# A hybrid encoder layer on one core: attention gates before the attention loop, memory queries and keys inside it, and the turn of the gates' maxima pinned within head 0

## The chip, the core and the metric

The kernel runs on one core of a Trainium2 chip. Its engines, as the profile names them, are PE (TensorE, the matrix multiplier), DVE (VectorE), ACT (ScalarE), POOL (GpSimd) and SP (SyncE, which here issues nearly all DMAs). Matmul results land in PSUM banks, all other tiles lie in SBUF. The metric is the device time of one execution in microseconds (us); the median of three is 2049.92.

## What is computed

Two sequences of 512 tokens, x_prompt and x_sample, of width 1024, go through the same layer in fp32. Cut to what matters here:

```python
x = x + 0.5 * swiglu(rms_norm(x, ffn1_norm), ffn1_w_gate, ffn1_w_up, ffn1_w_down)
h = rms_norm(x, mix_norm)
aq, ak, av, mq, mk, mv, gate_pre, o_pre, g_att, g_mlstm = jnp.split(h @ w_in, split_at, axis=-1)
aq = apply_rope(rms_norm(aq.reshape(B, S, 8, 64), q_norm), cos, sin)   # 8 heads
ak = apply_rope(rms_norm(ak.reshape(B, S, 2, 64), k_norm), cos, sin)   # 2 key heads
att = gqa_block_attention(aq, ak, av)                                  # softmax(q k / 8) v
mem = mlstm_bidirectional(mq, mk, mv, gate_pre, mlstm_gate_bias, o_pre, mlstm_head_norm)  # 4 heads of 128
merged = sigmoid(g_att) * (att @ w_up_att) + sigmoid(g_mlstm) * (mem @ w_up_mlstm)
x = x + merged @ w_out
x = x + 0.5 * swiglu(rms_norm(x, ffn2_norm), ffn2_w_gate, ffn2_w_up, ffn2_w_down)
```

The names to keep: **g_att** (attention gates, 8 blocks of 128 columns), **mq and mk** (memory queries and keys, 4 heads), **o_pre** (output gates, 4 heads) and **gate_pre** (16 columns of input and forget gates, from which running maxima are taken). `mlstm_bidirectional` is a gated linear attention in both directions, here computed in blocks of 128 tokens with those maxima as stabilizers.

## The kernel before

**Arithmetic.** A product of two fp32 matrices is made of three matmuls on pairs (hi, lo): hi x hi, hi x lo, lo x hi. So every operand that comes out of a computation is *split* (L712 to L714): ACT copies it to hi, DVE subtracts hi from it to get lo.

**Stages.** The first feed-forward network (both sequences), then `mix(s, ...)` (L837) once for each *stream* s: s=0 is x_prompt, s=1 is x_sample. Then the second network and the final norm. `mix` is a generator; the main program runs the first stream up to its output projection, starts the second stream's first projections, and lets the rest of the first stream's output projection run while the second stream prepares its queries. The tiles of mixing are 128 rows (columns of a weight) by 512 tokens.

**Units.** Nearly all projections of `mix` are *units* of 24 matmuls (8 blocks of the width times 3), each with 128 columns of w_in: `out_gate(h)` for o_pre, `att_gate(d)` for g_att, `mem_gate(d)` for g_mlstm, `mem_qk(h, j)` for mq (j=0) and mk (j=1). What follows a unit's last matmul differs:

- `mem_qk`: in the first stream DVE multiplies by R, the norm's factor of each token (L1013), then a split (ACT copy, DVE L714). In the second stream the input is already normed, and the split reads PSUM directly. The result lies in a tile of tag w8 in the first stream (the buffers of split weights, 4 of them) and of tag wr in the second (the buffers of weights as they come from memory, 4 of them).
- the gates (`gate_of`, L858 to L861): in the first stream DVE multiplies by R (L860), then ACT takes tanh; in the second ACT alone. An attention gate is written into `mg[:, d, :]`. The blocks `mg[:, 4:8, :]` hold the raw queries until these are turned, so gates 4 to 7 come after the last query turn.

**Weights.** `load_w` (L284): in the first stream a weight is fetched (L271), split by ACT (L278) and DVE (L279, one instruction of 128 x 1024), and both halves are written back to memory (*parked*, L301). In the second stream the parked halves are read (L293) and nothing is split. One unit's weights are always loaded ahead of its matmuls: `go` and `among` hold the next unit (`held`) while they compute one.

**From the queries to the attention loop.** After the projections of keys, values and queries stands the first yield of `mix`; between it and the second come `gates()` (L945: log-sigmoids, cumulative sums, one transpose, running maxima on DVE), the rotation of the first queries, `k_turn` (keys transposed by PE into a PSUM bank, then copied and subtracted by ACT and DVE, L928 to L931), `q_turn(0)` (L1029) and `gate_tops` (L982 to L986): two small transposes by PE of the maxima, 32 rows each (L984, L985), copied to SBUF by DVE. Turns take their bank from one pool of two (tile name pst). Around these stand four units, one before the first yield, three after the second.

**The attention loop.** 8 heads (h) of four steps (b). `score` (L1079) makes 128 x 512 scores with two matmuls, DVE takes the row maximum (L1086), ACT the exponential, DVE the reciprocal (L1089), and DVE or ACT scales the row (L1093, L1091). `turn_keys` (L1096) transposes a 128-column block of the four score tiles by four PE transposes (L1099) and splits the result. `values` (L1106) multiplies with the values. The scores of head h+1 are made while head h is turned, the values one step behind. In between, `among(n)` runs n matmuls of units one by one from the queue:

```python
if h + 1 < HA:
    nxt.append(score(h + 1, b))
among(FILLER[0])            # 5
pp = turn_keys(Ps, b)
among(FILLER[1])            # 3
if last:
    values(*last)
```

Four times `FIRST` = 9 matmuls of units stand between the first four scores.

**What sets the order.** Inside the loop scores, turns, values and the units' matmuls are *pinned* (`pin`, program order). Everything else is placed by the framework's scheduler, by priority: earlier code first, moved by `shifted(...)`. So an unpinned operation can move up or down past others when its inputs are ready, and the order of each engine comes out of that.

**After the loop.** The queue's rest runs (`fill(99)`), then four memory heads: `mem_head` (L1234 scores, L1248 weights by the maxima on DVE), `mem_out` (turns L1276, products L1284), with `merge_att` units and, behind heads 0 and 1, the queue entries of L1306. Then `mem_gate`, `merge_mem` and the output projection (`out_unit`, L1317; it reads the stream's input back from memory, f<-xbuf, L1322). In the first stream's loop hooks also load and norm the second stream's input (`prep1`, L1643).

Of the kernel before, what the change touches and what calls it, by code (L numbers as in the profile page):

```python
# [16 lines left out]
P = 128  # L17
S = 512
D = 1024
KD = D // P  # L20
# [6 lines left out]
def encoder(ctx, tc, I, outs):  # L27
    nc = tc.nc
# [13 lines left out]
    def nm(s):  # L42
        n_id[0] += 1
        return f"{s}_{n_id[0]}"
# [71 lines left out]
    def PT():  # L116
        return pt.tile([P, S], F32, tag="t", name=nm("pst"))

    def f(ap):
        return ap.bitcast(F32)  # L120
# [5 lines left out]
    ident = cpool.tile([P, P], F32, name="ident")  # L126
# [7 lines left out]
    def A(shape, dtype=F32, name="a"):  # L134
        return apool.tile(shape, dtype, tag="a", name=nm(name))
# [150 lines left out]
    def load_w(view, key):  # L286


        if key in parked:
            d, shape = parked[key]  # L290
            w2 = wpool.tile(shape, F32R, tag="w8", bufs=4, name=nm("w"))
            for i in range(2):
                nc.sync.dma_start(f(w2[:, i]), d[:, i])  # L293
            return w2[:, 0], w2[:, 1]
        raw = fetch_w(view)
        with shifted(-WEIGHTS):
            hi, lo = split_w(raw, V_)
        shape = [P, 2] + list(raw.shape[1:])
        parked[key] = d, _ = dpool.tile(shape, F32, name=nm("wpark")), shape
        for i, t in enumerate((hi, lo)):  # L300
            nc.sync.dma_start(d[:, i], f(t))  # L301
        return hi, lo
# [408 lines left out]
    def split(src, hi, lo, eng=None):  # L711

        nc.scalar.activation(hi, src, AF.Copy)  # L713
        (eng or V_).tensor_tensor(lo, src, f(hi), op=ALU.subtract)  # L714
# [53 lines left out]
    def go(*units):  # L768
        for load, comp in units:
            held.append((comp, load()))  # L770
            while len(held) > 1:
                c, w = held.pop(0)
                c(w)
# [6 lines left out]
    def tok_proj(xh, xl, cols, kk, done, banks):  # L780

        N = sum(n for _, n in cols)
        p = []

        def load(k0):
            return load_w([win_v[:, k0:k0 + kk, c:c + n] for c, n in cols], ("in", cols[0], k0))

        def comp(k0, w):
            wh, wl = w
            if not p:  # L790
                p.extend(b() for b in banks)
            for kl in range(kk):
                k = k0 + kl
                for b in range(4):
                    bs = slice(b * P, (b + 1) * P)
                    for i, (a, w_) in enumerate(((xh, wh), (xh, wl), (xl, wh))):
                        nc.tensor.matmul(p[b][:, :N], a[:, k, bs], w_[:, kl, :],  # L797
                                         start=(k == 0 and i == 0), stop=(k == KD - 1 and i == 2))
            if k0 + kk == KD:
                done(p)  # L800

        return [(lambda k0=k0: load(k0), lambda w, k0=k0: comp(k0, w)) for k0 in range(0, KD, kk)]

    def proj(view, key, src, n, done):

        def comp(w):
            done(proj_w(*w, src, n))

        def steps(w):
            p = []  # L810

            def step(k, i):
                if not p:
                    p.append(MM())
                (wh, wl), (sh, sl) = w, src(k)
                a, b = ((wh, sh), (wh, sl), (wl, sh))[i]
                pin(nc.tensor.matmul(p[0], a[:, k, :], b, start=(k == 0 and i == 0), stop=(k == n - 1 and i == 2)))  # L817
                if k == n - 1 and i == 2:
                    done(p[0])
            return [lambda k=k, i=i: step(k, i) for k in range(n) for i in range(3)]  # L820

        comp.steps = steps
        return (lambda: load_w(view, key)), comp
# [13 lines left out]
    def mix(s, xh, xl, early=None, extra=None, after=None):  # L837

        xsrc = lambda k: (xh[:, k, :], xl[:, k, :])
        queue = []  # L840

        def fill(n):
            go(*queue[:n])
            del queue[:n]

        def F2(dtype=F32):
            return T2(dtype, "f2")
# [10 lines left out]
        def gate_of(t, p):  # L858
            if not s:
                V_.tensor_tensor(t, p, R[s], op=ALU.mult)  # L860
            nc.scalar.activation(t, t if not s else p, AF.Tanh, scale=0.5)  # L861

        def win_cols(c0, done):
            return proj(win_v[:, :, c0:c0 + P], ("in", c0), xsrc, KD, done)
# [28 lines left out]
        def pair_turn(o, keep):  # L893
            p = PT()
            for b in range(4):
                keep(nc.tensor.transpose(p[:, b * P:(b + 1) * P], o[:, b, :], ident))
            return p

        qT = A([P, HA, S], F32R, "qT")
        mg = A([P, KD, S], F32, "mg")  # L900
# [80 lines left out]

        def gate_tops(run, top):  # L982
            p = PT()
            nc.tensor.transpose(p[:, 0:32], run, ident[0:32, 0:32])  # L984
            nc.tensor.transpose(p[:, 32:64], top.to_broadcast([32, P]), ident[0:32, 0:32])  # L985
            V_.tensor_copy(st[:, 0:2], p[:, 0:64].rearrange("p (i d b h) -> p i d b h", i=2, d=2, b=4))  # L986


# [13 lines left out]
        def mem_qk(h, j):  # L1002
            def done(pp):
                if j == 0 and not s:
                    t = wpool.tile([P, 4, S], F32R, tag="w8", bufs=4, name=nm("qk"))
                    qks[h] = [t[:, i] for i in range(4)]
                elif s:
                    t = wpool.tile([P, 2, S], F32R, tag="wr", bufs=4, name=nm("qk"))
                    qks.setdefault(h, []).extend(t[:, i] for i in range(2))
                t = pp  # L1010
                if not s:
                    t = F2()
                    V_.tensor_tensor(t, pp, R[s], op=ALU.mult)  # L1013
                split(t, *qks[h][2 * j:2 * j + 2])
            return win_cols((768, 1280)[j] + h * P, done)
# [3 lines left out]
        def out_gate(h):  # L1019
            def done(pp):  # L1020
                og = T2(F32, "ac")
                gate_of(og, pp)
                ogs[h] = og
            return win_cols(2320 + h * P, done)

        def q_rope(pr):
            return rope_steps(qraw[:, :, pr * P:(pr + 1) * P], rq[0][:, :, 2 * pr:2 * pr + 2], tabs[0])

        def q_turn(pr, keep):  # L1029
            p = pair_turn(qraw[:, :, pr * P:(pr + 1) * P], keep)  # L1030
            for h, own, other in ((2 * pr, lower, upper), (2 * pr + 1, upper, lower)):
                nc.scalar.activation(qT[own, h, :], p[own, :], AF.Copy)
                V_.tensor_tensor(qT[other, h, :], p[own, :], f(qT[own, h, :]), op=ALU.subtract)

        go(*tok_proj(xh, xl, [(512, 256), (2304, 16)], 2, kv_done, (PS, PS, MM, MM)))
        if early:
            early()
        go(*tok_proj(xh, xl, [(0, 512)], 2, q_done, (MM, PO, MM, MM)), mem_qk(0, 0))
        yield None
        tops = gates()  # L1040
        list(q_rope(0))
        with shifted(60):
            k_turn()
            q_turn(0, lambda i: i)
        gate_tops(*tops)
        yield None
        go(mem_qk(0, 1), mem_qk(1, 0), mem_qk(1, 1))

        def mem_rows(h, d):

# [86 lines left out]
                    between.extend(c.steps(w))  # L1137
                between.pop(0)()

        def att_gate(d):  # L1140
            def done(pp):
                gate_of(mg[:, d, :], pp)
            return win_cols(2832 + d * P, done)

        queue.extend(att_gate(d) for d in range(4))
        queue.extend(out_gate(h) for h in range(HM))
        queue.extend(att_gate(d) for d in range(4, 6))
        if not s:
            fill(1)
        Ps = []  # L1150
# [6 lines left out]
        for h in range(HA):  # L1157
            nxt = []
            for b in range(4):
                if h in (0, 2, 4) and b == 2:  # L1160
                    q_turn(h // 2 + 1, pin)
                if (h, b) in ((0, 3), (2, 3)):
                    rope = q_rope(h // 2 + 2)
                if h < 4:
                    next(rope, None)
                if h + 1 < HA:
                    nxt.append(score(h + 1, b))
                among(FILLER[0])
                pp = turn_keys(Ps, b)
                among(FILLER[1])  # L1170
                if last:
                    values(*last)
                last = h, b, pp
                if extra and b == 2 and h in (2, 3, 4):
                    extra[h - 2]()
            Ps = nxt
# [121 lines left out]
        for h in range(HM):  # L1298
            Ts = mem_head(h)
            if h == 0:  # L1300
                go(*mem_values())
            queue.append(merge_att(2 * h))
            fill(1)
            mem_out(h, Ts)
            if h + 2 < HM:
                queue.extend([att_gate(h + 6), mem_qk(h + 2, 0), mem_qk(h + 2, 1)])  # L1306
            queue.append(merge_att(2 * h + 1))
            fill(99)

# [25 lines left out]
    pin = tc.keep_in_program_order  # L1335
# [514 lines left out]
```

## Time and profile before

| what | value |
|---|---|
| time, median of 3 (lowest, highest) | 2049.92 us (2049.87, 2052.99) |
| the profiled execution: its time, its span | 2050.04 us, 2048.3 us |
| mean granted clock of TensorE | 0.999 |
| first network up to the loop's stage | 0 to 683 us |
| attention loop of the first stream, first score to last values | 705.4 to 814.5 us |
| memory heads of the first stream, products | 835.4 to 924.3 us |
| attention loop of the second stream, last values | 1189.8 us |
| memory heads of the second stream, products | 1213.9 to 1296.6 us |

How to read it: the span is what the profiler sees between first and last instruction; the execution's own time is 1.7 us longer, and sums are made against it. A row of the timeline gives start, duration, engine, source line, operation, output <- input, shape and count, and in brackets the idle time ahead of it with what ended it. A row of groups gives count, busy time and mean duration in ns. Line numbers are those of the kernel before; behind the edited places the changed kernel's lines lie a few numbers later or earlier (L1099 is L1103 there).

### The profile page before, as it was taken

The page shows a single profiled execution, that of the slowest core. Times are in us where ns is not written, and L with a number is a line of the kernel's source. Part 1 is how long each engine was busy: PE and PEld are TensorE (multiplying, and loading weights), DVE is VectorE, ACT ScalarE, POOL GpSimd, SP SyncE. Part 2 cuts the span into 40 slices and gives each one's busy share as a digit, 9 for nine tenths or more (in the row PEclk, how much of TensorE's full clock was granted, in tenths as well). Part 3 has the DMA queues.
Part 4 walks back from the last instruction along what each step waited for, and adds up shares of the span by engine and source line. Part 5 has one row for each costly group of instructions (what it writes and reads, how often), then busy time and mean ns, then how long its engine had stood idle before and what let it go on. Part 6 is the DMA issues. An engine that isn't in the chain of part 4 may idle for free.

```text
span 2048.3 us, 26765 instructions
## 1 busy us (share of the span) xinstructions
PE 2032.9 (99%) x9317; PEld 1678.7 (82%) x9317; DVE 1564.0 (76%) x2772; ACT 901.6 (44%) x1647; POOL 93.1 (5%) x116
## 2 busy tenths in 40 slices
PE   9999999999999999999999999999999999999998
PEld 7888888888888878888878888888888888888887
DVE  8888888886797888786566746446788988786797
ACT  7644444442234567563324553324444444442224
POOL 0000000001003000100120000001000000000001
PEclk9999999999999999999999999999999999999999
DMA  9656566799766853868684345677655655599753
GB/s 318 199 168 224 176 201 195 243 344 351 262 224 225 289 165 126 274 227 286 202 316 157 113 141 188 217 260 253 195 185 186 198 173 185 199 344 344 273 200 119
DMA packets 311014, 457.96 MB, mean 224 GB/s; under 512 B 20232, under 2 KB 182112, under 8 KB 309600
## 3 DMA queue, kind: packets, MB, share of 16 engines
q1 hardware_dynamic: 308800, 450.27, 65.2%
q0 software_dynamic: 1920, 5.72, 0.8%
q8 instruction: 73, 1.20, 0.2%
q14 instruction: 61, 0.50, 0.1%
q10 hardware_dynamic: 160, 0.27, 0.0%
HBM read 288.25 MB, written 167.94 MB: 223 GB/s over the span
## 4 chain that ended last, share of the span: by engine, by line
PE 94%; DVE 3%; ACT 1%; DMA 1%; issue 0%; SPq 0%; ACTq 0%; DVEq 0%
PE mm L830 15%; PE pst L372 12%; PE pso L372 12%; PE mm L372 10%; PE mm L630 8%; PE pss L372 6%; PE mm L817 5%; PE pss L630 4%; PE pst L630 4%; PE mm L797 4%; PE pso L630 3%; PE pso L1110 1%; PE pss L1083 1%; PE pst L1099 1%; PE pso L1284 1%; PE pss L1234 1%
## 5 line engine op out<-in xcount | busy, mean ns | idle before, releaser
L372 PE MATMUL pst<-xc,w 128*128 128x512 f32 x1056 | 253.6, 389 | 0.0
L372 PEld LDWEIGHTS pst<-xc,w 128*128 128x128 f32 x1056 | 198.2, 188 | 41.1
L372 PE MATMUL mm<-xc,w 128*128 128x512 f32 x972 | 229.6, 390 | 0.5 <-ACT f L380 0.5
L372 PEld LDWEIGHTS mm<-xc,w 128*128 128x128 f32 x972 | 182.0, 188 | 38.4 <-ACT f L380 0.9
L630 PE MATMUL mm<-rt,w 128*128 128x512 f32 x765 | 178.7, 389 | 0.0
L830 PE MATMUL mm<-xh,w 128*128 128x512 f32 x560 | 176.2, 392 | 0.0
L630 PEld LDWEIGHTS mm<-rt,w 128*128 128x128 f32 x765 | 143.5, 188 | 29.8
L330 ACT ACTIVATE w<-t 128x512 fp32r<-128x512 f32 x176 | 106.5, 627 | 135.7 <-issue 63.1
L331 DVE TENSOR_TENSOR w<-t,w 128x512 fp32r<-128x512 f32 x176 | 117.7, 687 | 41.5 <-ACT w L330 39.9
L372 PE MATMUL pss<-xc,w 128*128 128x512 f32 x528 | 126.8, 389 | 0.0
L372 PE MATMUL pso<-xc,w 128*128 128x512 f32 x528 | 126.8, 389 | 0.0
L372 PE MATMUL pso<-xc,f 128*128 128x512 f32 x528 | 126.8, 389 | 0.0
L830 PEld LDWEIGHTS mm<-xh,w 128*128 128x128 f32 x560 | 104.9, 188 | 21.5
L372 PEld LDWEIGHTS pso<-xc,f 128*128 128x128 f32 x528 | 99.1, 188 | 20.6
L372 PEld LDWEIGHTS pss<-xc,w 128*128 128x128 f32 x528 | 99.1, 188 | 20.6
L372 PEld LDWEIGHTS pso<-xc,w 128*128 128x128 f32 x528 | 99.1, 188 | 20.6
L817 PE MATMUL mm<-xh,w 128*128 128x512 f32 x336 | 114.6, 401 | 0.0
L830 PE MATMUL mm<-xl,w 128*128 128x512 f32 x280 | 109.7, 392 | 0.0
L713 ACT ACTIVATE w<-wr 128x512 fp32r<-128x512 f32 x72 | 45.1, 632 | 137.2 <-PE pso L630 71.8
L713 ACT ACTIVATE w<-t 128x512 fp32r<-128x512 f32 x82 | 51.8, 632 | 107.4 <-PE pst L630 62.4
L630 PE MATMUL pss<-rt,w 128*128 128x512 f32 x396 | 93.7, 389 | 0.0
L630 PE MATMUL pst<-rt,w 128*128 128x512 f32 x396 | 93.7, 389 | 0.0
(440 smaller groups left out, 4005.6 us busy)
## 6 DMA issues: line engine op xcount, KB each, us to landing
rt<-rbuf SPq DMA_DIRECT2D x154, 512.0 KB, 5.4
wpark<-w SPq DMA_DIRECT2D x104, 512.0 KB, 3.5
w<-wpark SPq DMA_DIRECT2D x104, 512.0 KB, 4.9
wr<-in_ffn_w_gate_dram SPq DMA_DIRECT2D x62, 512.0 KB, 5.4
rbuf<-tab SPq DMA_DIRECT2D x102, 256.0 KB, 3.9
wr<-in_ffn_w_up_dram SPq DMA_DIRECT2D x44, 512.0 KB, 4.5
rbuf<-f SPq DMA_DIRECT2D x72, 256.0 KB, 4.1
wr<-in_w_in_dram SPq DMA_DIRECT2D x36, 512.0 KB, 6.4
```

What stands on the lines that cost most here:

```text
L330: pin(nc.scalar.activation(t[:, 0], src, AF.Copy))
L331: pin(V_.tensor_tensor(t[:, 1], src, f(t[:, 0]), op=ALU.subtract))
L372: nc.tensor.matmul(p, a[:, k, :], xt[:, b, k, :], start=(first and k == 0 and i == 0), stop=(k == HK_ - 1 and i == 2), skip_group_check=True)
L630: nc.tensor.matmul(p, u[:, a, d * P:(d + 1) * P], r[:, b, ts], start=(first and q == 0 and k == 0), stop=(q == len(us) - 1 and k == 2), sk ...
L713: nc.scalar.activation(hi, src, AF.Copy)
L797: nc.tensor.matmul(p[b][:, :N], a[:, k, bs], w_[:, kl, :], start=(k == 0 and i == 0), stop=(k == KD - 1 and i == 2))
L817: pin(nc.tensor.matmul(p[0], a[:, k, :], b, start=(k == 0 and i == 0), stop=(k == n - 1 and i == 2)))
L830: nc.tensor.matmul(p, a[:, k, :], b, start=(k == 0 and i == 0), stop=(k == n - 1 and i == 2))
L1083: pin(nc.tensor.matmul(p, qT[:, h, b * P:(b + 1) * P], kv[:, hk * 2 + j, :], start=(j == 0), stop=(j == 1)))
L1099: pin(nc.tensor.transpose(p[:, b * P:(b + 1) * P], Ps[b][:, kb * P:(kb + 1) * P], ident))
L1110: pin(nc.tensor.matmul(pos[h], Vst[:, kb, h // 4, :], w, start=(kb == 0 and i == 0), stop=(kb == 3 and i == 1)))
L1234: nc.tensor.matmul(p, qk[a][:, isl], qk[b], start=(n == 0), stop=(n == 2))
```

## The change

In both streams the four units around the rotation, `mem_qk(0, 0)`, `(0, 1)`, `(1, 0)` and `(1, 1)`, become `att_gate(0)` to `att_gate(3)`. The loop's queue, before `att_gate` 0 to 3, `out_gate` 0 to 3, `att_gate` 4 and 5, becomes `out_gate` 0 to 3, the four `mem_qk`, `att_gate` 4 to 7. The gates 6 and 7 thereby leave the queue of the memory heads 0 and 1. `gate_tops` is called inside the loop at step (h=0, b=1), and its two transposes are pinned there. No matmul is added or removed.

```diff
@@ -981,8 +981,8 @@
 
         def gate_tops(run, top):
             p = PT()
-            nc.tensor.transpose(p[:, 0:32], run, ident[0:32, 0:32])
-            nc.tensor.transpose(p[:, 32:64], top.to_broadcast([32, P]), ident[0:32, 0:32])
+            pin(nc.tensor.transpose(p[:, 0:32], run, ident[0:32, 0:32]))
+            pin(nc.tensor.transpose(p[:, 32:64], top.to_broadcast([32, P]), ident[0:32, 0:32]))
             V_.tensor_copy(st[:, 0:2], p[:, 0:64].rearrange("p (i d b h) -> p i d b h", i=2, d=2, b=4))
 
 
@@ -1023,6 +1023,11 @@
                 ogs[h] = og
             return win_cols(2320 + h * P, done)
 
+        def att_gate(d):
+            def done(pp):
+                gate_of(mg[:, d, :], pp)
+            return win_cols(2832 + d * P, done)
+
         def q_rope(pr):
             return rope_steps(qraw[:, :, pr * P:(pr + 1) * P], rq[0][:, :, 2 * pr:2 * pr + 2], tabs[0])
 
@@ -1035,16 +1040,15 @@
         go(*tok_proj(xh, xl, [(512, 256), (2304, 16)], 2, kv_done, (PS, PS, MM, MM)))
         if early:
             early()
-        go(*tok_proj(xh, xl, [(0, 512)], 2, q_done, (MM, PO, MM, MM)), mem_qk(0, 0))
+        go(*tok_proj(xh, xl, [(0, 512)], 2, q_done, (MM, PO, MM, MM)), att_gate(0))
         yield None
         tops = gates()
         list(q_rope(0))
         with shifted(60):
             k_turn()
             q_turn(0, lambda i: i)
-        gate_tops(*tops)
         yield None
-        go(mem_qk(0, 1), mem_qk(1, 0), mem_qk(1, 1))
+        go(att_gate(1), att_gate(2), att_gate(3))
 
         def mem_rows(h, d):
 
@@ -1137,14 +1141,9 @@
                     between.extend(c.steps(w))
                 between.pop(0)()
 
-        def att_gate(d):
-            def done(pp):
-                gate_of(mg[:, d, :], pp)
-            return win_cols(2832 + d * P, done)
-
-        queue.extend(att_gate(d) for d in range(4))
         queue.extend(out_gate(h) for h in range(HM))
-        queue.extend(att_gate(d) for d in range(4, 6))
+        queue.extend(mem_qk(h, j) for h in range(2) for j in range(2))
+        queue.extend(att_gate(d) for d in range(4, KD))
         if not s:
             fill(1)
         Ps = []
@@ -1159,6 +1158,8 @@
             for b in range(4):
                 if h in (0, 2, 4) and b == 2:
                     q_turn(h // 2 + 1, pin)
+                if (h, b) == (0, 1):
+                    gate_tops(*tops)
                 if (h, b) in ((0, 3), (2, 3)):
                     rope = q_rope(h // 2 + 2)
                 if h < 4:
@@ -1303,7 +1304,7 @@
             fill(1)
             mem_out(h, Ts)
             if h + 2 < HM:
-                queue.extend([att_gate(h + 6), mem_qk(h + 2, 0), mem_qk(h + 2, 1)])
+                queue.extend([mem_qk(h + 2, 0), mem_qk(h + 2, 1)])
             queue.append(merge_att(2 * h + 1))
             fill(99)
```

## The prediction

> **What bounds the kernel now.** I read the page first: busy time of each engine, then the chain of work that ended last.
>
> ```profile
> span 2048.3 us, 26765 instructions
> PE 2032.9 (99%) x9317; PEld 1678.7 (82%) x9317; DVE 1564.0 (76%) x2772; ACT 901.6 (44%) x1647; POOL 93.1 (5%) x116
> PE 94%; DVE 3%; ACT 1%; DMA 1%; issue 0%; SPq 0%; ACTq 0%; DVEq 0%
> ```
>
> PE (TensorE) is busy for all but 15.4 us of the span, and the chain is PE for 94%. The change alters no matmul, so only moments at which PE stands still can be won or lost. One matmul of 512 columns costs the distance between starts, not its shown 0.39 us:
>
> ```profile
> 971.24 2.88 PE L830 MATMUL pss<-mem,w 128*128 128x512 f32 x12
> 973.96 2.88 PE L830 MATMUL pst<-mem,w 128*128 128x512 f32 x12
> ```
>
> (973.96 - 971.24) / 12 = 0.227 us. So a stall costs the idle time that a row shows plus 0.39 - 0.23 = 0.16 us, by which a shown matmul overlaps the next. The view of PE's waits has these in the mixing stage:
>
> ```profile
> PE pst L984 <- DVE kv L931: 1.5, 1, 1.5
> PE pss L797 <- DVE t L1215: 0.8, 1, 0.8
> PE pst L1099 <- ACT t L1091: 0.7, 1, 0.7
> PE pst L1099 <- DVE t L714: 0.6, 2, 0.3
> PE pst L1099 <- DVE t L1093: 0.4, 1, 0.4
> PE pst L1099 <- DVE qT L1033: 0.3, 1, 0.3
> ```
>
> All but the second belong to code that the change touches: the gate turn (L984) and the key turns of the attention loop (L1099).
>
> **The change, part by part.** Times are made against the profiled execution, 2050.04 us (span 2048.3), 0.12 above the median of 2049.92.
>
> *The gate turn.* In the second stream it costs most. From the timeline:
>
> ```profile
> 1045.34 1.23 DVE L279 TENSOR_TENSOR w<-wr,w 128x1024 fp32r<-128x1024 f32 x1 [2.72 <-DMA f<-xbuf]
> 1048.77 0.69 DVE L929 TENSOR_TENSOR kv<-pst,kv 64x512 fp32r<-64x512 f32 x1
> 1049.13 0.39 PE L830 MATMUL mm<-mh,w 128*128 128x512 f32 x1
> 1049.49 0.69 DVE L1323 SCALAR_TENSOR_TENSOR f<-mm,f 128x512 f32<-128x512 f32 x1
> 1050.22 0.69 DVE L931 TENSOR_TENSOR kv<-pst,kv 64x512 fp32r<-64x512 f32 x1
> 1051.06 0.22 PE L984 MATMUL pst<-ident,f 32*128 32x32 f32 x1 [1.54 <-DVE kv L931]
> ```
>
> L984 wants the bank that the key turn filled, and its last reader L931 is late on DVE (VectorE), behind a weight split and a load. Behind L984 stands every later matmul of PE. The loss is 1.54 + 0.16 = 1.70 us. In the first stream the same turn costs (698.44 - 697.73) - 2 x 0.227 = 0.26 us:
>
> ```profile
> 697.73 0.61 PE L830 MATMUL mm<-xh,w 128*128 128x512 f32 x2
> 698.44 0.21 PE L984 MATMUL pst<-ident,f 32*128 32x32 f32 x1
> ```
>
> The order of PE in the second stream before (mm_9147 is an output projection of the first stream):
>
> ```order
> L830 MATMUL mm_9147<-mh_8042,w_9101 128x512 x2
> L830 MATMUL mm_9147<-ml_8043,w_9101 128x512
> L830 MATMUL mm_9147<-mh_8042,w_9101 128x512
> L984 MATMUL pst_9055<-ident,f_1057_9022 128x32
> L985 MATMUL pst_9055<-ident,f_1057_9022 128x32
> L830 MATMUL mm_9147<-mh_8042,w_9101 128x512
> ```
>
> and with the change, behind the first key turn of head 0 (L1103 is L1099 of before, L1087 the next scores):
>
> ```order
> L1103 MATMUL pst_9447<-ident,t_1100_9352 128x128
> L1103 MATMUL pst_9447<-ident,t_1105_9375 128x128
> L1103 MATMUL pst_9447<-ident,t_1108_9394 128x128
> L1103 MATMUL pst_9447<-ident,t_1113_9418 128x128
> L817 MATMUL mm_9409<-xh_8371,w_9357 128x512 x2
> L817 MATMUL mm_9409<-xl_8372,w_9357 128x512
> L984 MATMUL pst_9459<-ident,f_1056_9020 128x32
> L985 MATMUL pst_9459<-ident,f_1056_9020 128x32
> L1087 MATMUL pss_9463<-kv_8556,qT_8559 128x512 x2
> ```
>
> There it takes the bank of the query turn, read long before. L931 is next wanted by the first scores, which in the profile begin far behind it:
>
> ```profile
> 1081.32 0.62 PE L1083 MATMUL pss<-kv,qT 128*128 128x512 f32 x2
> ```
>
> So both losses go: 1.70 + 0.26 = 1.96 us. What is late next: the following key turn must reuse the bank of the turn just before it. That is a wait of the kind that the query turns already make in heads 0, 2 and 4:
>
> ```profile
> 718.80 0.69 DVE L714 TENSOR_TENSOR t<-pst,t 128x512 fp32r<-128x512 f32 x1
> 723.72 0.40 PE L817 MATMUL mm<-xh,w 128*128 128x512 f32 x1
> 724.26 0.66 PE L1099 MATMUL pst<-ident,t 128*128 128x128 f32 x4
> 754.02 0.63 PE L1099 MATMUL pst<-ident,t 128*128 128x128 f32 x4 [0.29 <-DVE qT L1033]
> 778.61 0.63 PE L1099 MATMUL pst<-ident,t 128*128 128x128 f32 x4 [0.31 <-DVE t L714]
> 1099.75 0.52 PE L1099 MATMUL pst<-ident,t 128*128 128x128 f32 x3 [0.31 <-DVE t L714]
> ```
>
> They cost 0.54 - 0.23 = 0.31, 0.45, 0.47 and 0.47 us. The new place costs between nothing and twice 0.47; I take 0.1, since at 718.80 DVE reads the first turn for the last time, ends at 719.49, and the next turn comes at 724.26.
>
> *Units exchanged in the rotation stage.* Four mem_qk leave, four att_gate come: 24 matmuls each, no difference on PE. On DVE, rows of the groups in 683 to 706:
>
> ```profile
> L1013 DVE TENSOR_TENSOR f<-mm,R 128x512 f32<-128x512 f32 x4 | 2.7, 685 | 0.0
> L714 DVE TENSOR_TENSOR qk<-f,qk 128x512 fp32r<-128x512 f32 x3 | 2.1, 687 | 0.0
> L279 DVE TENSOR_TENSOR w<-wr,w 128x1024 fp32r<-128x1024 f32 x3 | 3.7, 1217 | 0.0
> ```
>
> A mem_qk of the first stream needs two of the first two kinds, an att_gate one (L860, of the same size), so four L714, 2.75 us, leave; in the second stream an att_gate needs none. DVE's order in the first stream, about the first two scores (L1086, L1090 after), before:
>
> ```order
> L1013 TENSOR_TENSOR f_462_5859<-mm_5834,R_5146 128x512
> L1086 TENSOR_REDUCE asm_5866<-pss_5863 128x1
> L279 TENSOR_TENSOR w_5875<-wr_5873,w_5875 128x1024
> L714 TENSOR_TENSOR qk_5820<-f_462_5859,qk_5820 128x512
> L1089 RECIPROCAL asm_5866<-asm_5866 128x1
> L1086 TENSOR_REDUCE asm_5894<-pss_5891 128x1
> ```
>
> and now:
>
> ```order
> L860 TENSOR_TENSOR mg_5279<-mm_5822,R_5146 128x512
> L1090 TENSOR_REDUCE asm_5852<-pss_5849 128x1
> L279 TENSOR_TENSOR w_5993<-wr_5991,w_5993 128x1024
> L1093 RECIPROCAL asm_5852<-asm_5852 128x1
> L1090 TENSOR_REDUCE asm_5880<-pss_5877 128x1
> ```
>
> The split L714 is gone from between. Counted to the fourth score, DVE has four L714 less and one L279 more (weights split sooner): 2.75 - 1.22 = 1.5 us earlier. That matters, as DVE is full there:
>
> ```profile
> 705.00:735.00 30.00, 29.48 (x143) 23.94 (x142) 29.00 (x66) 19.28 (x38) 0.00 (x0) 1.00 0.67 223
> 735.00:760.00 25.00, 23.99 (x120) 19.39 (x120) 20.40 (x38) 18.01 (x36) 0.00 (x0) 1.00 0.49 159
> 760.00:780.00 20.00, 19.69 (x101) 15.96 (x100) 18.03 (x43) 14.85 (x30) 0.00 (x0) 1.00 0.46 158
> ```
>
> (us, then PE, PE's loads, DVE, ACT, POOL busy, clock, DMA share, GB/s.) DVE works 29.0 of 30 us, and the first key turn waits for its last softmax row, 0.38 + 0.16 = 0.54 us:
>
> ```profile
> 717.80 0.33 PE L1099 MATMUL pst<-ident,t 128*128 128x128 f32 x1 [0.38 <-DVE t L1093]
> 758.48 0.33 PE L1099 MATMUL pst<-ident,t 128*128 128x128 f32 x1 [0.72 <-ACT t L1091]
> ```
>
> 1.5 us cover that 0.54, and 0.2 of the 0.31 at 724. I take 0.74; bounds 0 and 0.85.
>
> *Units in the loop.* PE takes 4 x 9 + 32 x 8 + 5 = 297 steps there. Before, 10 units (240 steps) in the first stream and 11 (264) in the second; now 12 (288) and 13 (312). The tail of head 7 was filled with memory matmuls that the scheduler pulled forward and is now filled by units: nothing won, since PE did not wait there. The mem_qk come in heads 2 to 4, where 754.02, 758.48 and 778.61 wait (0.45, 0.88, 0.47); each adds 0.69 us to DVE there. Bounds: all four exposed, +2.75; the three waits and the one at 1099.75 gone, -2.27. DVE has 4.6 of 25 and 2.0 of 20 us free, and it enters ahead, so I take 0.
>
> *Units taken out of the memory heads.* Two att_gate no longer stand between heads 0, 1 and 2 of each stream, 24 x 0.227 = 5.4 us of PE work each. Their cover is the rest of the stage:
>
> ```profile
> 837.50:857.50 20.00, 20.00 (x90) 16.35 (x89) 14.09 (x26) 9.96 (x27) 4.41 (x3) 1.00 0.80 241
> ```
>
> Without the unit DVE has 14.09 - 1.22 - 0.69 = 12.2 us to do in 14.6: it still fits. Nothing; uncovered it would cost up to 5.4 us a head.
>
> *DMAs.* The memory's query and key tiles of the second stream lie in the buffers of raw weights (tag wr). As they come later, SP fetches the output weights sooner, past the second stream's first weights. SP before:
>
> ```order
> L271 DMA wr_8875<-in_w_out_dram 128x8x128
> L301 DMA wpark_8435<-w_8432 128x1024 x2
> L301 DMA wpark_8487<-w_8484 128x1024 x2
> L293 DMA w_8564<-wpark_5289 128x544
> L1643 DMA f_973_8477<-xbuf_102 128x512
> ```
>
> and now:
>
> ```order
> L271 DMA wr_8909<-in_w_out_dram 128x8x128
> L301 DMA wpark_8435<-w_8432 128x1024 x2
> L271 DMA wr_8948<-in_w_out_dram 128x8x128
> L301 DMA wpark_8487<-w_8484 128x1024 x2
> L271 DMA wr_9053<-in_w_out_dram 128x8x128
> L293 DMA w_8564<-wpark_5289 128x544
> L1644 DMA f_959_8373<-xbuf_102 128x512
> ```
>
> ```profile
> 965.00:970.00 5.00, 5.00 (x24) 4.14 (x23) 4.09 (x6) 3.07 (x6) 1.47 (x2) 1.00 0.52 143
> 970.00:982.00 12.00, 12.00 (x55) 9.93 (x54) 12.00 (x16) 4.37 (x7) 5.32 (x4) 1.00 0.65 215
> 1054.00:1087.00 33.00, 33.00 (x148) 27.31 (x147) 12.31 (x19) 8.26 (x14) 6.13 (x7) 1.00 1.00 347
> 967.67 0.42 SPq L293 DMA_DIRECT2D w<-wpark  x1
> 983.41 0.52 PE L797 MATMUL pss<-w,xh 128*128 128x272 f32 x2 [0.76 <-DVE t L1215]
> ```
>
> Three fetches of 128 x 8 x 128 floats are 1.57 MB, 4.5 us at the 347 GB/s that the last row shows with the DMA engines full. The first weights were issued at 967.67, and the projection that reads them waits at 983.41 for something else: 15 us of room. The input tiles (f<-xbuf) have less, as DVE, which reads them, is full from 970 to 982; but 0.48 and 0.35 of the engines' time is free then. I take 0; bounds 0 and 4.5. The Trainium skill says of this ("DMA: Bandwidth & Descriptors", section "Issuing engines are not separate DMA queues") that transfers run on the same 16 engines and interleave, whoever issues them. By that rule the later loads do not simply queue behind the three fetches but share with them from the first byte, which speaks against the change: 4.5 us in place of my 0.
>
> Sum: -1.96 + 0.1 - 0.74 = -2.6 us; 2050.04 - 2.6 = **2047.4 us**.
>
> **The rivals.** *All waits on DVE in the two loops go.* DVE's lead of 1.5 us and more would also cover 754, 758, 778 and 1099: 1.96 + 0.54 + 0.31 + 2.27 = 5.08, so 2045.0 us. For it: the lead is larger than each wait. Against: two of them come from the turn of a bank within one step of the loop, which a lead does not lengthen.
>
> *The memory heads of the first stream lose their cover (slower).* The turns of the memory weights (L1276) wait for DVE, behind them all of PE. Price 5.4 us for each of two heads: 2047.4 + 10.9 = 2058.3 us. It decides for slower from 6.6 us of the 10.9 on. Against: the 2.4 us that are free in the row of 837.5.
>
> *The transfers.* The input tiles come 4.5 us late in 970 to 982, DVE stands, the projection at 983 waits: half of it exposed gives 2049.7, all 2051.9 us. For it: DVE is full there and is the releaser at 983.41; against: the free DMA time.
>
> **How the numbers follow.** About 0.2% (4.1 us: below 2045.8, above 2054.0) is what a measurement of this kernel tells from no change. Chances: forecast 0.52, all waits go 0.28, heads uncovered 0.10, transfers 0.10. The forecast's own range is 2045.5 to 2050.0 (one mem_qk in the loop or one wait either way, and the new bank wait). Faster: the 0.28 and 0.05 of the forecast's edge, 0.33. Slower: 0.10 and 0.02 for transfers beyond the bound, 0.12. Within: 0.55. The range must take in the second case with the wait at 983 partly gone (2044.2) and the transfers to their full price (2051.9, rounded up); only the heads stay outside.
>
> **What would show it.** Right: no wait of L984 on DVE left in the view of PE's waits; no idle time before the first key turn of the first stream; PE's idle time smaller by some 2 us; waits of L1103 on L714 in heads 2 to 4 still there. Wrong: idle time before L1277 (the memory turns), before the second stream's L797 over 1 us, a new wait of the second key turn in head 0, or ACT and DVE waiting for w<-wr longer than the 2.72 us at 1045.

## The result, and the profile after

The changed kernel takes 2056.02 us (median of 10 runs, 2055.06 to 2059.51) against 2050.26 before in the same runs: ratio **1.0026**, 95% interval 1.0016 to 1.0036. It is slower by 5.8 us, where 2.6 us less was forecast. From the page of the changed kernel, these are the span, the busy times and the engines' shares of the chain:

```profile
span 2053.9 us, 26759 instructions
PE 2034.7 (99%) x9317; PEld 1679.4 (82%) x9317; DVE 1563.4 (76%) x2772; ACT 902.1 (44%) x1647; POOL 92.4 (4%) x116
PE 90%; DVE 5%; ACT 2%; DMA 2%; issue 1%; SPq 0%; DVEq 0%; ACTq 0%
```

PE does the same 9317 matmuls; the chain has lost 4% of PE to other engines. The view of PE's waits in the mixing stage of the changed kernel (who waits, for whom; us in total, times, longest):

```profile
PE pss L1235 <- DVE t L1251: 3.6, 4, 1.7
PE pst L1103 <- DVE t L714: 1.3, 2, 1.0
PE pso L1114 <- DVE t L714: 1.0, 1, 1.0
PE pss L797 <- DVE t L1216: 0.8, 1, 0.8
PE pst L1103 <- ACT t L1095: 0.7, 1, 0.7
PE pst L896 <- DVE mg L891: 0.3, 1, 0.3
PE pst L971 <- DVE fa L969: 0.3, 1, 0.3
PE pso L1114 <- DVE f L1126: 0.2, 1, 0.2
```

The gate turn (L984) is off the list, as forecast. At the list's head stands a line that was not there before: **the scores of the memory heads (L1235, L1234 before) wait for DVE's L1251**, which reads the scores before them out of the same bank. By place, each number the sum of distances between matmul starts beyond the usual pitch (0.227 us at 512 columns, 0.109 at the turns' 128), in us:

| place | before | after |
|---|---|---|
| rotation of the first stream (L984, then L896) | 0.26 | 0.48 |
| attention loop, first stream | 2.67 | 4.08 |
| memory heads, first stream | 0 | 1.62 |
| rotation of the second stream (L984, then L971) | 1.70 | 0.47 |
| attention loop, second stream | 0.48 | 0 |
| memory heads, second stream | 0 | 2.82 |

Together +4.4 of the 5.6 us between the two spans. Another 0.7 arose in the first network, where both kernels do the same (the matmuls of L797 on `mm` begin at 647.8 in place of 647.1); some 0.5 us is spread over gaps too small to tell.

How a memory head loses its cover is best seen in the second stream, at head 1. Timeline of the changed kernel:

```profile
1239.53 0.69 DVE L1060 TENSOR_TENSOR box<-box,tab 128x512 f32<-128x512 f32 x1 [5.06 <-DMA box<-ebuf]
1241.64 0.69 DVE L1060 TENSOR_TENSOR box<-box,tab 128x512 f32<-128x512 f32 x1 [0.74 <-DMA box<-ebuf]
1244.11 1.52 PE L1235 MATMUL pss<-qk,qk 128*128 128x512 f32 x6
1246.74 0.69 DVE L714 TENSOR_TENSOR mem<-box,mem 128x512 fp32r<-128x512 f32 x1 [0.70 <-ACT mem L713]
1247.95 0.28 DVE L1251 SCALAR_TENSOR_TENSOR t<-pss,t 128x128 f32<-128x128 f32 x1
1248.91 0.50 PE L1235 MATMUL pss<-qk,qk 128*128 128x512 f32 x1 [1.69 <-DVE t L1251]
```

and of the kernel before:

```profile
1236.26 1.52 PE L1234 MATMUL pss<-qk,qk 128*128 128x512 f32 x6
1237.09 0.69 DVE L714 TENSOR_TENSOR qk<-mm,qk 128x512 fp32r<-128x512 f32 x1 [2.96 <-ACT qk L713]
1238.76 0.85 PE L1234 MATMUL pss<-qk,qk 128*128 128x512 f32 x3
```

Between two memory heads DVE works off a chain in a fixed order: head 0's norm (short operations on `row`, each on the result of the one before), its product and its split (`mem`), and only then L1251 of head 1. Before, DVE was through with it early and stood idle for 2.96 us until PE had made the next unit. With 24 matmuls (5.4 us) taken from between the heads PE arrives first; DVE still adds the mask rows (L1060, late because of their load) and runs the chain, and PE, after two banks of scores, waits.

The loads of the mask rows have a share in this wait that no run measured. DVE stands 5.06 and 0.74 us for them, and its order puts the first addition ahead of the norm and the second one inside it:

```profile
1238.65 0.29 PE L232 MATMUL pst<-row,fold 128*128 128x16 f32 x2
1240.74 0.16 DVE L235 TENSOR_SCALAR row<-pst 128x16 f32<-128x16 f32 x1
```

PE has made the norm's input at 1238.94, but L235 starts 1.8 us later, and the second addition holds the norm for 1.3 us more. With the rows added in the idle time before, L1251 would come up to 3 us sooner (an estimate from these rows), more than the 1.69 that PE waits. So the missing units are the cause that the next runs show; rows that come sooner may be another remedy, and were not tried here.

In the first stream a collision adds to it. At head 2 of the changed kernel:

```profile
892.84 1.47 POOL L1060 TENSOR_TENSOR box<-box,tab 128x512 f32<-128x512 f32 x1 [0.54 <-DMA box<-ebuf]
893.08 2.31 DVE L279 TENSOR_TENSOR w<-wr,w 128x1024 fp32r<-128x1024 f32 x1
896.36 0.93 PE L1235 MATMUL pss<-qk 128*128 128x512 f32 x3 [0.78 <-DVE t L1251]
```

The weight split, 1.22 us in the median, takes 2.31 while POOL adds, until 1.08 us after POOL has ended. The Trainium skill ("SBUF — State Buffer", section "SBUF: two separate sides") has one pair of ports for both engines, locked for a whole instruction when DVE has two inputs in SBUF; the rows agree with it. That this collision makes this one wait was not tried by itself.

### The profile page after: what moved, and what is told of

Its sections match the earlier page's. It is cut to its first block, busy times and chain, and to the rows that moved or that the text cites. A ratio compares the mean times of both kernels' runs of the same rounds, so it can differ in the third digit from the quotient of the medians.

```text
span 2053.9 us, 26759 instructions
## 1 busy us (share of the span) xinstructions
PE 2034.7 (99%) x9317; PEld 1679.4 (82%) x9317; DVE 1563.4 (76%) x2772; ACT 902.1 (44%) x1647; POOL 92.4 (4%) x116
## 4 chain that ended last, share of the span: by engine, by line
PE 90%; DVE 5%; ACT 2%; DMA 2%; issue 1%; SPq 0%; DVEq 0%; ACTq 0%
PE pst L372 12%; PE pso L372 12%; PE mm L830 11%; PE mm L372 10%; PE mm L630 8%; PE pss L372 6%; PE mm L817 5%; PE pst L630 4%; PE pss L630 4%; PE mm L797 4%; PE pso L630 3%; PE pso L1114 1%; PE pst L1103 1%; PE pss L1087 1%; PE pso L1285 1%; PE pso L797 1%
## 5 line engine op out<-in xcount | busy, mean ns | idle before, releaser
L830 PEld LDWEIGHTS mm<-xh,w 128*128 128x128 f32 x496 | 93.0, 188 | 18.9
L830 PE MATMUL mm<-xl,w 128*128 128x512 f32 x248 | 97.3, 392 | 0.0
```

The source lines that it names most:

```text
L830: nc.tensor.matmul(p, a[:, k, :], b, start=(k == 0 and i == 0), stop=(k == n - 1 and i == 2))
```

## The experiments

**Gates 6 and 7 put back behind the memory heads** (gates_back). As the changed kernel, but:

```diff
-        queue.extend(att_gate(d) for d in range(4, KD))
+        queue.extend(att_gate(d) for d in range(4, 6))
...
-                queue.extend([mem_qk(h + 2, 0), mem_qk(h + 2, 1)])
+                queue.extend([att_gate(h + 6), mem_qk(h + 2, 0), mem_qk(h + 2, 1)])
```

> The changed kernel with gates 6 and 7 put back behind memory heads 0 and 1; all else as changed. Theory (lost cover): the waits of the memory scores (L1235) on DVE L1251 in the changed kernel, 0.44 + 0.24 + 0.94 us in the first stream and 1.85 + 0.97 in the second, go, because 24 matmuls again stand between the heads: 2056.0 - 4.4 = 2051.6 us, and the view of PE's waits names L1235 no more. Rival (the memory's queries and keys in the loop delay what the heads need): the waits stay, 2055.5 to 2056.5 us.

Measured 2051.36 us, 1.0000 of the kernel before (0.9991 to 1.0009). The three largest of its waits of PE, and DVE ahead of L1251 at head 1 of the second stream:

```profile
PE pst L1103 <- DVE t L714: 1.6, 2, 1.3
PE pso L1114 <- DVE t L714: 1.0, 1, 1.0
PE pss L797 <- DVE t L1216: 0.8, 1, 0.8
```

```profile
1238.71 0.69 DVE L714 TENSOR_TENSOR qk<-mm,qk 128x512 fp32r<-128x512 f32 x1 [2.82 <-ACT qk L713]
```

L1235 stands nowhere in the view, DVE's idle time ahead of the split is back, and with that, within the interval, the whole loss is gone. Lost cover holds; by the trace, what is left of the change costs about as much in the first stream (waits of 4.9 us in place of 2.9) as it wins in the second (0.5 in place of 2.2).

**Gate 7 alone put back** (gate7_back).

```diff
-        queue.extend(att_gate(d) for d in range(4, KD))
+        queue.extend(att_gate(d) for d in range(4, 7))
...
-                queue.extend([mem_qk(h + 2, 0), mem_qk(h + 2, 1)])
+                queue.extend(([att_gate(7)] if h else []) + [mem_qk(h + 2, 0), mem_qk(h + 2, 1)])
```

> Only gate 7 put back, behind memory head 1; gate 6 stays in the loop. Lost cover: the waits at head 1's scores stay (0.44 and 1.85 us), those at head 2's go (1.18 and 0.97): 2056.0 - 2.15 = 2053.9 us. If the two gates were only needed as a sum (any work anywhere between the heads): all or none of 4.4 us goes, 2051.6 or 2056.

Measured 2054.68 us, 1.0021 (1.0012 to 1.0030). The median lies between the two, but the interval overlaps that of the changed kernel (1.0016 to 1.0036), so the trace has to tell (its execution, 2052.82 us, was the shortest of the eleven). It shows what was expected: two waits left of four, both at head 1.

```profile
PE pss L1235 <- DVE t L1251: 2.1, 2, 1.9
```

By these rows each gate covers its own pair of heads; it is not a matter of the sum.

**The exchange without the turn's move** (units_only). `gate_tops` unpinned and in its old place behind the first query turn.

```diff
             q_turn(0, lambda i: i)
+        gate_tops(*tops)
...
-                if (h, b) == (0, 1):
-                    gate_tops(*tops)
```

> The exchange of units alone; the turn of the maxima stands unpinned in its old place. Theory (the turn's move is worth what was forecast): the wait of L984 is back, 1.70 + 0.26 us, 2056.0 + 1.96 = 2058.0 us; a part of the new waits before it (L971 on DVE 0.47, L896 on DVE 0.48) may be in it, then 2057. Rival (the move is worth nothing, since the wait only goes to the next turn): 2056.0 us.

Measured 2059.26 us, 1.0037 (1.0024 to 1.0050): near the number expected, but not for the reason. L984 waits only 0.18 us beyond its pitch in the second stream, so the exchange alone takes that wait away. The time lies elsewhere:

```profile
PE pss L1234 <- DVE t L1250: 4.2, 4, 2.2
PE pst L1104 <- DVE t L714: 2.8, 2, 2.4
```

```profile
725.06 0.69 DVE L1061 TENSOR_TENSOR box<-box,tab 128x512 f32<-128x512 f32 x1 [2.49 <-DMA box<-ebuf]
726.41 0.66 PE L1104 MATMUL pst<-ident,t 128*128 128x128 f32 x4 [2.44 <-DVE t L714]
```

The first fence is PE's waits (L1234 is the memory scores, L1104 the key turns), the second the timeline at the third key turn of head 0: DVE stands for a load of mask rows with the turn's split queued behind it. The changed kernel has the same there, 0.93 us of DVE and 0.97 of PE. Some 1.4 us more pass at half the clock behind the wait of 2.2 us (last section). What the turn's move is worth beside the exchange stays open: the intervals of 1.0037 and 1.0026 overlap.

**The turn's move without the exchange** (turn_only).

```diff
         def gate_tops(run, top):
...
-            nc.tensor.transpose(p[:, 0:32], run, ident[0:32, 0:32])
-            nc.tensor.transpose(p[:, 32:64], top.to_broadcast([32, P]), ident[0:32, 0:32])
+            pin(nc.tensor.transpose(p[:, 0:32], run, ident[0:32, 0:32]))
+            pin(nc.tensor.transpose(p[:, 32:64], top.to_broadcast([32, P]), ident[0:32, 0:32]))
...
-        gate_tops(*tops)
...
+                if (h, b) == (0, 1):
+                    gate_tops(*tops)
```

> The kernel before with the turn of the maxima pinned at step 1 of head 0 and no unit exchanged. Theory: 2050.3 - 1.96 + 0 to 0.5 (the bank of the next key turn) = 2048.3 to 2048.8 us, no wait of L984 on DVE. Rival (the new place costs: the wait at the third key turn of head 0, 0.3 us before and 1.15 in the changed kernel, is the turn's doing): that wait is 1.15 again and the time 2049.1 us or more.

Measured 2050.86 us, 1.0000 (0.9991 to 1.0008): no gain that can be told. The third key turn has no long wait, so the rival's reason falls as well. The first line of its waits and the timeline show what came instead:

```profile
PE mm L830 <- DMA w<-wpark: 1.7, 2, 1.2
```

```profile
1070.33 0.47 PE L830 MATMUL mm<-xh,w 128*128 128x512 f32 x1 [0.56 <-DMA w<-wpark]
1072.20 0.74 PE L830 MATMUL mm<-xh,w 128*128 128x512 f32 x2 [1.17 <-DMA w<-wpark]
```

The stretch of 1042 to 1078 us, first of the kernel before, then of the turn alone, then of the next experiment (columns as in the prediction; the last two are the DMA engines' share and GB/s):

```profile
1042.00:1078.00 36.00, 34.46 (x155) 28.12 (x155) 16.78 (x30) 11.64 (x17) 9.83 (x11) 1.00 1.00 352
```

```profile
1042.00:1078.00 36.00, 34.27 (x146) 27.46 (x145) 14.15 (x18) 11.48 (x16) 9.84 (x11) 0.95 0.99 349
```

```profile
1042.00:1078.00 36.00, 36.00 (x164) 29.64 (x163) 14.05 (x21) 9.85 (x15) 9.82 (x11) 1.00 0.83 281
```

In both of the first two the DMA engines are full for 36 us. PE, no longer held at L984, runs into weights that are not there yet. The profiled execution, 2053.88 us, was the longest of the eleven (median 2050.86), so its trace shows a dearer case than most; but the same wait stands in the profile of first_only below, which lies at that kernel's median. The move has one more price in the second stream: the third key turn of head 0, which waited 0.48 us beyond its pitch before, now waits 0.88.

```profile
1103.67 0.63 PE L1098 MATMUL pst<-ident,t 128*128 128x128 f32 x4 [0.70 <-DVE t L714]
```

**The exchange in the second stream alone, and in the first alone** (second_only, first_only). Gates 6 and 7 behind the memory heads, the turn moved in both; `s` picks the old or the new units (`not s` for the complement):

```diff
+        go(*tok_proj(...), att_gate(0) if s else mem_qk(0, 0))
...
+        go(*([att_gate(1), att_gate(2), att_gate(3)] if s else [mem_qk(0, 1), mem_qk(1, 0), mem_qk(1, 1)]))
...
+        if not (s):
+            queue.extend(att_gate(d) for d in range(4))
         queue.extend(out_gate(h) for h in range(HM))
+        if s:
+            queue.extend(mem_qk(h, j) for h in range(2) for j in range(2))
```

> Units exchanged in the second stream alone (gates 6 and 7 behind the memory heads as before); the first stream's units as before; the maxima's turn pinned in both. Theory (the exchange costs in the first stream, where DVE is full, and gains in the second, where the output weights then come sooner and leave the DMA engines room): first stream as before without its gate turn, -0.3 to -0.5; second stream 0.47 us of waits in place of 1.70 + 0.48, -1.7: some 2.2 us below the kernel before, 2048.8, DMA share under 0.95 in the 30 us before the second loop and no wait of L830 on w<-wpark. Rival (time won before the second loop always goes to the DMA): 2050.5 to 2051, with such a wait.

> The complement: units exchanged in the first stream alone, gates 6 and 7 behind the memory heads, turn pinned in both. Theory: the first stream's waits 4.9 in place of 3.0 us, the second stream as with the turn alone (gate turn won, as much lost to late w<-wpark, DMA share about 1): some 2 us above the kernel before, 2053. Rival (parts do not add, the loss came from gates 6 and 7 only): as before, 2051.

Second stream alone: 2050.22 us, 0.9991 (0.9982 to 1.0000). First stream alone: 2056.15 us, 1.0021 (1.0013 to 1.0030). The directions are as expected; the loss with the first stream's exchange is larger than the 2 us expected. By its trace, the first stream waits 5.2 us in place of 2.9, about as expected, but the second does not break even: 4.0 in place of 2.2. Beside w<-wpark (2.1) it has two waits of 0.4 and 0.6 us for DVE's weight splits (L279) and the 0.88 of the third key turn. The two versions add up to 1.0012, where both together (gates_back) gave 1.0000: within their intervals, but not proof that the parts add. PE's waits with the second stream alone:

```profile
PE pss L797 <- DVE t L1219: 0.8, 1, 0.8
PE pst L1103 <- ACT t L1095: 0.7, 1, 0.7
PE pst L971 <- DVE fa L969: 0.3, 1, 0.3
PE pst L1103 <- DVE t L714: 0.3, 1, 0.3
PE pst L1103 <- DVE qT L1038: 0.3, 1, 0.3
PE pst L1103 <- DVE t L1097: 0.2, 1, 0.2
```

and, with the first stream alone, the line that the turn's move had brought:

```profile
PE mm L830 <- DMA w<-wpark: 1.7, 2, 1.0
```

With the exchange in the second stream the output weights are fetched ahead, the DMA engines have room (0.83; 0.95 in first_only), and nothing waits for w<-wpark.

**The first mask rows loaded early** (rows_early). As gates_back, with the loads of box<-ebuf for memory head 0 written behind `gates()`:

```diff
         tops = gates()
+        rows0.extend(row_load(0, d) for d in range(2))
...
+            eb3, em3 = rows0.pop(0) if rows0 else row_load(h, d)
```

> As gates_back, with the loads of the first memory head's rows (box<-ebuf) written ahead of the units, so that SP issues them some 30 us sooner. Theory (the long wait at the third key turn of head 0 is DVE standing in order for that load): DVE's idle time on box<-ebuf near 724 us goes, the wait of the turn falls from 1.45 to 0.3 us or so, 2051.4 - 1.1 = 2050.3 us. Rival (the bank of the moved turn of the maxima makes it, or DVE is late there anyway): the wait stays above 1 us and the time at 2051.4.

Measured 2051.47 us, 0.9997 (0.9989 to 1.0006), as without it. The wait at the third key turn is gone, so DVE did stand there for that load; but two others have grown:

```profile
PE pst L896 <- DVE mg L891: 1.4, 1, 1.4
PE pst L1109 <- DVE t L1103: 0.6, 1, 0.6
```

DVE now meets the load 30 us sooner, before the rotation's last step (L891), and passes the delay to the query turn. With DVE as full as it is there, the wait that was removed came back at other places.

**The output weights not parked** (turn_unparked, second_unparked). The first stream does not write them back; the second fetches and splits them again. With the turn alone, and with the exchange in the second stream alone:

```diff
         with shifted(-WEIGHTS):
             hi, lo = split_w(raw, V_)
+        if key[0] == "out":
+            return hi, lo
```

> turn_only, but the first stream does not write its split output weights back to memory (8 x 1 MB less to write around 1020 to 1075 us); the second stream fetches and splits them again, behind 1300 us. Theory (the time won at the gate turn went to the DMA engines, which are full from 1042 to 1078): no wait of L830 on w<-wpark, DMA share in 1042 to 1078 under 0.95, and the gate turn's 1.7 us shows: 2050.9 - 1.7 to 2.0 = 2049 us, if the 8 splits in the second stream's output projection stay hidden. Rival (the late weights come from the order of SP's queue, not from full DMA engines): the wait on w<-wpark stays, 2050.9 us.

> second_only with the same output weights unparked. Theory: its DMA engines already had room (share 0.86 to 0.95), so there is nothing more to win before the second loop: as second_only, 0.9991 of the kernel before, within 0.5 us. Rival (DMA still costs there): a further 1 us or more.

With the turn alone 2053.61 us, 1.0009 (1.0000 to 1.0018); with the second stream's exchange **2049.19 us, 0.9989 (0.9980 to 0.9998)**, the lowest median of the study, though its interval overlaps that of the second stream's exchange with parked weights (0.9982 to 1.0000). In the first, the wait on w<-wpark is gone and the DMA share from 1042 to 1078 is 0.65, as the theory has it, but the gain is not to be seen: a new wait stands just before. First PE's wait (L973 and L971 are L971 and L969 elsewhere), then DVE's timeline:

```profile
PE pst L973 <- DVE fa L971: 2.7, 1, 2.7
```

```profile
1038.66 1.23 DVE L279 TENSOR_TENSOR w<-wr,w 128x1024 fp32r<-128x1024 f32 x1 [2.06 <-ACT w L278]
1039.80 1.25 DVE L971 TENSOR_TENSOR fa<-Is,cs 128x32 f32<-128x32 f32 x1
```

DVE stands for ACT's half of a late weight's split (ACT had waited 3.00 us for the fetch), and L971, whose result PE turns next, is queued behind. So the run does not decide between full DMA engines and the order of SP's queue: PE reaches the weights some 4 us later than it would have, longer than the 2.1 us that it had waited for them, and unparking takes entries out of SP's queue as well as bytes off the engines. The second version loses nothing, as expected.

## Why the prediction was wrong

- **Units taken out of the memory heads: the step that failed.** It took 0, because DVE's 12.2 us of work without the unit fit into the 14.6 us that remain. That was an average over a head's length, and of head 0. What matters is the order inside it: how long DVE stands idle just ahead of the operation that precedes L1250. That was 2.96 us at head 1 of the second stream, less than the 5.4 us taken away. The loss is 4.4 us (1.62 and 2.82), shown by gates_back, and falls on the scores, not on the turns where the rival and the last part looked for it. The idle time tells that a loss comes, but not its size: at heads 1 and 2 of the first stream and then of the second it was 0.66, 2.92, 2.96 and 2.79 us in the kernel before, so 5.4 less it gives 4.8, 2.5, 2.4 and 2.6, and measured are 0.44, 1.18, 1.85 and 0.97. The chain has other idle moments further up, which may take up a part. The rival, right about lost cover, took the whole unit as exposed in the first stream, 10.9 us, and left out the second.
- **The gate turn: right that the wait goes, wrong about the gain.** 1.96 was forecast. In the changed kernel turns before it wait instead (L971 0.47, L896 0.48), which leaves 1.01. These come with the exchange and not with the move: units_only has both, turn_only neither, and in units_only the exchange alone has cut the wait of L984 in the second stream to 0.18. By itself the move wins nothing that can be told. In its profile PE meets late weights, where the DMA engines are full; the row of 1054 to 1087 us, quoted for the DMA rate, said so already, with a share of 1.00.
- **The new bank wait** was taken as 0.1. The third key turn's wait rose from 0.31 to 1.15, not for the moved turn's bank but because DVE stood for box<-ebuf: units_only, where the turn is not moved, has the wait too (2.60), and turn_only has not. The exchange has SP issue that load some 30 us later, behind further weights; first the kernel before, then the changed one:

```profile
687.01 0.92 SPq L1053 DMA_DIRECT2D box<-ebuf  x2
```

```profile
717.08 1.73 SPq L1057 DMA_DIRECT2D box<-ebuf  x2
```

No part of the prediction followed this DMA.
- **Units exchanged in the rotation stage:** the wait of the first key turn is gone, 0.54 us, as forecast; the other 0.2 of that term, from the third key turn, did not come.
- **Units in the loop** was taken as 0. In the second stream the wait of 0.48 went. In the first the three waits of 753 to 778 us, 1.82 together, became four of 2.94: +1.1, within the bounds given. Which moved operation makes each of them was not tried.
- **DMAs** were taken as 0, with a loss as the only bound. The loss did not come: the second stream's L797 waits 0.76 us, as before. By the traces, fetching the output weights ahead is a part that wins: without it, as in first_only, PE waits 1.7 us on w<-wpark.

Added up from the table: gate turn -1.01, third key turn +0.84, first key turn -0.54, units in the loops +0.64, heads +4.44, together +4.4 us where -2.6 was forecast. The heads are over half of the miss.

## What to carry to other kernels

Slack is not the busy share of a window; look at the idle time of the one instruction that stands ahead of the awaited one in its engine's order, since a unit that looks free to move may be what gives it. It warns of a loss and does not price it. Before a stall is counted as won, look for the next thing that arrives no sooner: here DMA engines at a share of 1.00 for 36 us. On an engine that is full and works in order, as DVE did here, an instruction that waits for a load delays those behind it, so follow where a moved edit puts each load in its queue.

## What the runs showed of the hardware

After some stalls PE runs at half its clock for about 3 us. The windows behind a wait in three kernels: the exchange without the turn's move, after 2.2 us of idle PE; the turn alone with unparked weights, after 2.74; the turn alone, after 0.56 and 1.17 close together (the clock is the third number from the end).

```profile
1251.00:1254.00 3.00, 3.00 (x8) 2.32 (x9) 1.42 (x8) 0.00 (x0) 0.00 (x0) 0.50 0.00 0
```

```profile
1041.00:1044.00 3.00, 2.89 (x8) 2.32 (x9) 3.00 (x11) 0.00 (x0) 0.00 (x1) 0.50 0.08 21
```

```profile
1072.00:1076.00 4.00, 3.80 (x10) 3.02 (x11) 0.69 (x1) 0.00 (x0) 0.00 (x0) 0.61 1.03 418
```

A matmul of 512 columns then costs 0.427 us in place of 0.227, some 1.4 us in all, on top of the wait. It did not follow every long wait: none after 1.69 us in the changed kernel, nor after the 2.44 us at 726.41 above, nor in first_only after 0.71 and 1.04 us close together. The Trainium skill ("TensorE: Matmul & The Clock Gate", Part 1) has the clock halved after an idle window of about 3.4 us that runs freely; the stalls here were shorter than that.
